# Modulation chunks of the first and last attention layer in halves of 256 columns, one a step

## The chip, the cores and the metric

The kernel runs on one core of a Trainium2 chip. The metric is the device time of one execution in microseconds (us), as the median of several. Five engines work side by side, each through its own list of instructions: PE multiplies matrices, ACT (ScalarE) applies functions and copies, DVE (VectorE) and POOL (GpSimd) do elementwise work, SP (SyncE) issues the transfers (DMAs). They wait for each other only by semaphores. PE's results land in banks of PSUM, everything else lives in SBUF.

## The reference

Four layers over 512 latent and 256 context tokens of width 1024 (batch 1). Layer 0 and layer 3 are of the first kind (multi-head latent attention), layer 1 is a banded window attention (called layer B below), layer 2 a long convolution (layer C). Each layer is modulated by the condition:

```python
for layer in range(DEPTH):
    mx = cond_x @ w_mod[layer] + b_mod[layer]          # cond = silu(c), 1024 -> 3072
    mc = cond_c @ w_mod[layer] + b_mod[layer]
    shift_x, scale_x, gate_x = jnp.split(mx[:, None, :], 3, axis=-1)
    shift_c, scale_c, gate_c = jnp.split(mc, 3, axis=-1)
    hx = rmsnorm(x, g_pre[layer]) * (1.0 + scale_x) + shift_x
    hc = rmsnorm(ctx, g_pre[layer]) * (1.0 + scale_c) + shift_c
    yx, yc = mixer(hx, hc, ...)
    x = x + gate_x * rmsnorm(yx, g_post[layer])
    if with_ctx_out:                                   # not in the last layer
        ctx = ctx + gate_c * rmsnorm(yc, g_post[layer])
```

The mixer of the first kind begins with one projection `h @ w_in`, cut into four: `cq` (512 columns), `ckv` (256), `kr` (64) and a gate (1024). `cq` and `ckv` are normalized (rmsnorm) and multiplied further; the gate goes through SiLU.

## The kernel before

**Modulation.** `w_mod` of a layer is cut into chunks of 512 columns, c = 0 to 5, and each chunk into four blocks of 128x4x256 words, 512 KB each. A chunk is a unit of work: `mod_ab_unit` for scale and shift of the next layer (c = 0 to 3), `mod_g_unit` for the gate of this one (two of them). `mod_chunk` takes the four blocks one after another, does four matmuls for each (each reads 128x256 and writes 32 rows; in the trace a block is x8, a whole unit x32, at L442), all into one bank of PSUM. Then ACT copies the 512 columns out (L455 for scale and shift, L480 for the gate), and for scale and shift PE transposes the copy in four pieces (L459). The units wait in a list, `fillers`, and code of the layers calls `fill()` to put one in: its matmuls need no result of the layer, only their blocks.

**Staging.** Blocks come by two streams, `W` (weights of the layers) and `M` (modulation). `take` gives a block to its reader, and `pump` issues the DMAs of blocks ahead of their readers (L211, on SP's queue), as far as a slot of 1024 words is free in the arena `arena_f` and no more than `cap_d` blocks are staged. A block's slot is free again when its last matmul has read it. A block that isn't staged when its reader is written down is loaded then, into whatever is free. Weights are split into a high and a low part after landing (L230 on ACT, L233 on DVE or POOL), modulation blocks aren't. The low slots of the arena also hold the buffers of the layer (`og`, in layer B the probability buffers `prob` and `sums`), so where a layer's buffers are laid depends on which slots are taken at that moment.

**Layer of the first kind** (`layer_A`). A first loop runs over the six key tiles of 128 tokens: 24 matmuls of 320 columns (L577 to L579) into a bank, then `normed` for 256 of them. `normed` squares and sums on ACT (L715), takes the root and reciprocal in two POOL steps (L358, L359), scales on DVE (L718), transposes on PE (L721) and splits the result. The 64 columns of `kr` are rotated, copied (L757) and transposed (L761). A second loop runs over six cq tiles (four in layer 3): 24 matmuls of 512 columns, then `normed` for 512. A third runs over eight gate blocks, 24 matmuls (L588) for each of the two spans of tokens. Layer 0 has six units to place (four of layer 1's scale and shift, two of its own gate), layer 3 two. `UKS`, `UQ` and `UC` tell from which key tile, cq tile and gate one unit is placed before each step: layer 0 places its six at key tiles 3, 4, 5 and cq tiles 0, 1, 2, layer 3 its two at key tiles 4 and 5. From there on `cap_d` and `look_d` of `M` are 2.

**Order.** The instructions are written in the order of the loops; a scheduler, working from the written order and what each instruction depends on, then sets the order on each engine. What PE meets behind a tile, and so what covers the chain of `normed`, comes out of it. `self.a()` gives the next of a ring of four PSUM banks (pa), `wide` alternates two larger ones (pb).

Of the kernel before, what the change touches and what calls it, by code (L numbers as in the profile page):

```python
# [15 lines left out]
AF = mybir.ActivationFunctionType  # L16
# [4 lines left out]
D = 1024  # L21
# [7 lines left out]
AH = 2  # L29
SU = 2  # L30
WX = {25: (3, 2), 27: (3, 2), 29: (3, 3)}
UKS = (3, 4)
UQ = 0
UC = 0
MC = 2
CH = ((0, 384),)
LS = 2
WD = 3
# [97 lines left out]
class Ring:  # L136
# [6 lines left out]
    def next(self):  # L143
        self.i += 1
        return self.blocks[self.i % len(self.blocks)]
# [125 lines left out]
class Kern:  # L271
# [138 lines left out]
    def want_mod(self, unit):  # L410
        kind, L, c = unit
        w = self.io["w_mod"][L].rearrange("(k p) n -> p k n", p=P)
        if kind == "g":
            c += 4
        for kb in range(4):
            n0, k0 = 512 * c + 256 * (kb // 2), 4 * (kb % 2)
            self.M.want(("mod", L, c, kb), w[:, k0:k0 + 4, n0:n0 + 256], split=False)
# [27 lines left out]
            if kb < 3:  # L445
                yield

    def mod_ab_unit(self, L, c, bank=None):

        nc = self.nc  # L450
        bank = bank or self.a
        ps = bank()
        yield from self.mod_chunk(L, c, ps)
        m = self.fs(512)
        nc.scalar.activation(m.ap, ps, AF.Copy)  # L455
        yield
        ps = bank()
        for b in range(4):
            nc.tensor.transpose(ps[:, P * b:P * b + P], m.ap[:, P * b:P * b + P], self.ident)  # L459
        m.free()  # L460
        part, k0 = c // 2, 4 * (c % 2)
        r = self.col(8).rearrange("p (b s) -> p b s", b=4)
        nc.vector.tensor_reduce(r, ps.rearrange("p (b j s) -> p b s j", b=4, j=4)[:, :, 0:2, :], axis=AX.X, op=ALU.add)
        bm = self.bmod[:, L, 4 * c:4 * c + 4, None].to_broadcast([P, 4, 2])
        if part == 0:
            nc.vector.tensor_tensor(self.ab[:, L, 1, k0:k0 + 4], r, bm, op=ALU.add)
        else:
            nc.vector.scalar_tensor_tensor(r, r, 1.0, bm, op0=ALU.add, op1=ALU.add)
            nc.vector.tensor_tensor(self.ab[:, L, 0, k0:k0 + 4], r, self.gpre[:, L, k0:k0 + 4, None].to_broadcast([P, 4, 2]),
                                    op=ALU.mult)  # L470

    def mod_g_unit(self, L, c, bank=None):

        nc, io = self.nc, self.io
        ps = (bank or self.a)()
        yield from self.mod_chunk(L, 4 + c, ps)
        if c == 0:
            self.mg[L] = self.fs(D)
        m = self.mg[L].ap[:, 512 * c:512 * c + 512]
        nc.scalar.activation(m, ps, AF.Copy)  # L480
        nc.sync.dma_start(out=m[2:3, :], in_=io["b_mod"][L:L + 1, 2048 + 512 * c:2560 + 512 * c])
        yield

# [12 lines left out]
        m.free()  # L496
        return g

    def unit(self, bank=None):
        kind, L, c = self.fillers.pop(0)  # L500
        return (self.mod_ab_unit if kind == "ab" else self.mod_g_unit)(L, c, bank)

    def fill(self, n=1):
        for _ in range(n):
# [197 lines left out]
    def layer_A(self, L, j, h, ctx_out, last):  # L702
        nc, R, F = self.nc, self.R, self.F
# [8 lines left out]
        def normed(ps, n, dst, t):  # L712

            ssq = self.col()
            nc.scalar.activation(self.trash[:, 0:n], ps, AF.Square, accum_out=ssq)  # L715
            self.rstd(ssq, n)
            cn = self.fs(n)
            nc.vector.tensor_scalar(cn.ap, ps, ssq, None, op0=ALU.mult)  # L718
            pt = self.a()
            for k in range(n // P):  # L720
                nc.tensor.transpose(pt[:, P * k:P * k + P], cn.ap[:, P * k:P * k + P], self.ident)  # L721
            cn.free()
            self.split_ps(dst[:, 0, :, P * t:P * t + P], dst[:, 1, :, P * t:P * t + P],
                          pt[:, 0:n].rearrange("p (k n) -> p k n", n=P))

        UK = UKS[0 if ctx_out else 1]
        units = sum(f[:2] in (("ab", L + 1), ("g", L)) for f in self.fillers)

        wide = Banks(self.halves())
        ckv = self.rl(2 * 2 * T)  # L730
# [6 lines left out]
        self.W.pump(4, 3)  # L737
        wk = lambda k: (ws[k // 2][1][0][:, k % 2], ws[k // 2][1][1][:, k % 2])
        for t in order:
            if t == UK:  # L740
                self.M.cap_d = self.M.look_d = MC
            if units and t >= UK:
                self.fill()
                units -= 1
            ps = wide.next()
            self.mm_tok(ps[:, 0:320], h, t, wk, 320)
            normed(ps[:, 0:256], 256, ckvv, t)
            ks = small.next()
            kv4 = ks.v(2, 2, 64)
            if t < 4:  # L750
                kf = self.ropes.next()
                self.rope_ps(kf.v(1, 64), ps[:, 256:320].rearrange("p (a b) -> p a b", a=1), t, 1)
                src = kf.ap[:, 0:64]
            else:
                kf = None
                src = ps[:, 256:320]
            nc.scalar.activation(kv4[:, 0], src[:, None, :].to_broadcast([P, 2, 64]), AF.Copy)  # L757
            nc.vector.tensor_tensor(kv4[:, 1], src[:, None, :].to_broadcast([P, 2, 64]), kv4[:, 0].bitcast(F32), op=ALU.subtract)
            pt = self.a()
            for i in range(2):  # L760
                nc.tensor.transpose(pt[:, P * i:P * i + P], ks.ap[:, P * i:P * i + P].bitcast(F32), self.ident)  # L761
            nc.vector.tensor_copy(krv[:, :, P * t:P * t + P], pt[:, 0:256].rearrange("p (a b) -> p a b", a=2))
# [4 lines left out]
        cqv = cq.v(2, 4, TQ)  # L767
        ws = [self.W.take(("cq", k)) for k in range(0, KD, 2)]
        for t in (order if ctx_out else qt):
            if units and t >= UQ:  # L770
                self.fill()
                units -= 1
            ps = wide.next()
            self.mm_tok(ps, h, t, wk, 512)
            normed(ps, 512, cqv, t)
# [2 lines left out]

        spans = [(0, NX), (NX, NC)] if ctx_out else [(0, NX)]
        for c in range(8):  # L780
            if units and c >= UC:
                self.fill()
                units -= 1
            blk, (wh, wl) = self.W.take(("gate", c))
            outs = [self.a()[:, 0:n] for _, n in spans]
            self.mm_ch(outs, lambda part, k, i: self.h_at(h, part, k, *spans[i]), lambda k: (wh[:, k], wl[:, k]))
            blk.free()
            for (t0, n), o in zip(spans, outs):
                self.gate2(ogv[:, c, t0:t0 + n], o)
        for b in h:  # L790
            b.free()
        self.lo_pool = True
        self.M.cap_d = self.M.look_d = 1

# [152 lines left out]
        units = [(hd, t) for hd in range(8) for t in qt]  # L947
# [891 lines left out]
```

## Time and profile before

| | |
|---|---|
| median of 3 runs | 1951.43 us (1951.01 to 1953.01) |
| the profiled execution | 1952.31 us, span 1950.4 |
| mean granted clock of PE | 0.984 |
| busy: PE, DVE, ACT, POOL | 1818.6, 1169.7, 814.3, 519.7 us |
| waits of PE for modulation blocks in arena_f | 21.6 us in the whole span |
| layer 0's projections | 148 to 312 us |
| layer B's attention | 700 to 985 us |
| layer 3's projections | 1590 to 1715 us |

How to read the rows: a timeline row gives start, duration, engine, line, operation, tiles, shape and count of instructions in a run, and in brackets how long the engine stood idle before it and for what. A row of the waits gives the sum, how often, and the longest. A row of windows gives the window, its length, busy time and (count) of PE, of PE's weight loads, of DVE, ACT and POOL, then the granted clock of PE, the busy share of the DMA engines and GB/s. A row of groups gives the count, busy time and mean duration in ns, then the idle time of the engine before it and what ended it. Rows of SP give when a DMA was issued, and L211 is where both streams issue theirs.

### The profile page before, as it was taken

What the parts mean: (1) busy time and instruction counts of PE and PEld (TensorE: products, weight loads), DVE (VectorE), ACT (ScalarE), POOL (GpSimd) and SP (SyncE); (2) the same over time, 40 slices, a digit from 0 to 9 for tenths busy, and PEclk for the clock granted to TensorE, in tenths of its full rate; (3) what the DMA queues carried; (4) which work ended last, traced back from release to release, by engine and by line L of the source; (5) the groups of instructions that cost most, each with busy time, mean ns of one, the idle gap of its engine ahead of it and who ended that gap; (6) DMA issues with size and microseconds to landing.
All of it is one profiled execution on the core that took longest, in us unless ns stands there. A gap on an engine that the chain in (4) does not pass through costs nothing. (4 is left out here: it accounts for less than half of the span.)

```text
span 1950.4 us, 30304 instructions
## 1 busy us (share of the span) xinstructions
PE 1818.6 (93%) x11628; PEld 1576.9 (81%) x11628; DVE 1169.7 (60%) x2365; ACT 814.3 (42%) x1688; POOL 519.7 (27%) x523
## 2 busy tenths in 40 slices
PE   5879799999999899999989999999989899999998
PEld 3657588999988888888868789999988677889986
DVE  6694134777755277777665456655566553477663
ACT  3473132555544255665654522222222352354451
POOL 5561000000213321222231444444434221000120
PEclk9899999999999999999999999999999899999999
DMA  7867431010133122222363622222222334310121
GB/s 219 261 172 230 150 80 30 23 33 34 55 108 109 55 65 67 77 77 66 107 207 108 200 81 77 76 76 71 72 64 71 107 127 140 97 33 23 44 66 65
DMA packets 186356, 186.31 MB, mean 96 GB/s; under 512 B 16600, under 2 KB 164952, under 8 KB 186212
## 3 DMA queue, kind: packets, MB, share of 16 engines
q1 hardware_dynamic: 186212, 184.39, 30.6%
q8 instruction: 91, 1.49, 0.3%
q14 instruction: 53, 0.43, 0.1%
HBM read 160.24 MB, written 24.12 MB: 95 GB/s over the span
## 5 line engine op out<-in xcount | busy, mean ns | idle before, releaser
L588 PE MATMUL pb<-arena_r 128*128 128x512 f32 (+1 forms) x1488 | 280.9, 342 | 1.9 <-DVE arena_f L567 1.0
L341 ACT ACTIVATE arena_r<-pa 128x384 fp32r<-128x384 f32 (+2 forms) x382 | 175.5, 479 | 206.1 <-PE pa L909 67.9
L588 PEld LDWEIGHTS pb<-arena_r 128*128 128x128 f32 x1488 | 230.1, 190 | 32.9 <-ACT arena_r L1462 1.5
L342 DVE TENSOR_TENSOR arena_r<-pa,arena_r 128x384 fp32r<-128x384 f32 (+2 forms) x382 | 199.5, 536 | 81.7 <-ACT arena_r L341 79.8
L588 PE MATMUL pa<-arena_r,swing_R 128*128 128x512 f32 (+1 forms) x816 | 165.9, 355 | 0.6 <-DVE arena_r L342 0.4
L588 PEld LDWEIGHTS pa<-arena_r,swing_R 128*128 128x128 f32 x816 | 132.2, 188 | 21.8 <-DVE arena_r L342 0.6
L884 PE MATMUL pb<-arena_r 128*128 128x384 f32 (+1 forms) x720 | 141.5, 337 | 3.0 <-ACT arena_r L341 1.8
L606 PE MATMUL pb<-arena_r 128*128 128x512 f32 x552 | 133.7, 394 | 1.6 <-ACT arena_r L230 1.3
L233 POOL TENSOR_TENSOR swing_R<-arena_f,swing_R 128x1024 fp32r<-128x1024 f32 (+1 forms) x33 | 76.2, 2313 | 192.0 <-ACT swing_R L230 142.5
L884 PEld LDWEIGHTS pb<-arena_r 128*128 128x128 f32 x720 | 119.1, 188 | 5.1 <-ACT arena_r L341 2.5
L606 PEld LDWEIGHTS pb<-arena_r 128*128 128x128 f32 x552 | 102.5, 188 | 25.1 <-ACT arena_r L230 1.8
L679 POOL TENSOR_TENSOR arena_f<-arena_f 128x128 f32<-128x128 f32 (+1 forms) x44 | 20.9, 475 | 362.8 <-DVE small L892 178.6
L233 POOL TENSOR_TENSOR arena_r<-swing_F,arena_r 128x1024 fp32r<-128x1024 f32 x36 | 88.0, 2448 | 88.7 <-ACT arena_r L230 83.5
L358 POOL TENSOR_SCALAR small<-small 128x1 f32<-128x1 f32 x68 | 17.8, 261 | 348.0 <-ACT trash L564 139.5
L923 PE MATMUL pa<-arena_r 128*128 128x256 f32 x624 | 91.5, 286 | 2.1 <-DVE arena_r L342 2.1
L923 PEld LDWEIGHTS pa<-arena_r 128*128 128x128 f32 x624 | 81.9, 189 | 4.8 <-ACT arena_r L341 2.5
L1079 PE MATMUL pa<-swing_R,arena_r 128*128 128x256 f32 x576 | 80.3, 289 | 5.0 <-DVE arena_f L348 3.8
L230 ACT ACTIVATE arena_r<-swing_F 128x1024 fp32r<-128x1024 f32 x39 | 41.4, 1063 | 103.9 <-PE pb L588 63.3
L888 DVE TENSOR_REDUCE small<-pb 128x1 f32<-128x768 f32 (+1 forms) x80 | 67.5, 845 | 21.6 <-PE pb L884 20.7
L891 ACT ACTIVATE arena_f<-pb,small 128x768 f32<-128x768 f32 (+1 forms) x80 | 65.2, 817 | 33.1 <-DVE small L889 26.7
L1079 PEld LDWEIGHTS pa<-swing_R,arena_r 128*128 128x128 f32 x576 | 72.9, 192 | 7.3 <-DVE arena_f L348 5.2
L442 PE MATMUL pa<-arena_f,cst 128*32 128x256 f32 x744 | 56.7, 405 | 21.7 <-DMA arena_f<-in_w_mod_dram 21.6
(268 smaller groups left out, 4210.0 us busy)
## 6 DMA issues: line engine op xcount, KB each, us to landing
arena_f<-in_w_mod_dram SPq DMA_DIRECT2D x93, 512.0 KB, 4.7
swing_F<-in_c_w_in_dram SPq DMA_DIRECT2D x31, 512.0 KB, 5.0
kd<-arena_f SPq DMA_DIRECT2D x48, 256.0 KB, 3.5
arena_f<-in_a_w_in_dram SPq DMA_DIRECT2D x24, 512.0 KB, 3.7
arena_f<-kd SPq DMA_DIRECT2D x16, 768.0 KB, 5.2
arena_f<-in_b_w_in_dram SPq DMA_DIRECT2D x20, 512.0 KB, 3.7
x<-arena_f SPq DMA_DIRECT2D x18, 512.0 KB, 4.2
arena_f<-in_a_w_out_dram SPq DMA_DIRECT2D x16, 512.0 KB
```

The source lines that it names most:

```text
L230: nc.scalar.activation(hi, view, AF.Copy)
L233: eng.tensor_tensor(lo, view, hi.bitcast(F32), op=ALU.subtract)
L341: self.nc.scalar.activation(hi, src, AF.Copy)
L342: self.nc.vector.tensor_tensor(lo, src, hi.bitcast(F32), op=ALU.subtract)
L442: nc.tensor.matmul(ps[32 * j:32 * j + 32, n0:n0 + 256], self.cst[:, 4 * kh + j, :], w[:, j, :], start=(kh == 0), stop=(kh == 1), skip_grou ...
L588: nc.tensor.matmul(out, l, rhs(part, k, i), start=(k == 0 and q == 0), stop=(k == kt - 1 and q == 2))
L606: nc.tensor.matmul(ys[:, 512 * hf:512 * hf + 512], ov[:, a, k - ks.start], wt[:, 0, 512 * hf:512 * hf + 512], start=(k == 0 and q == 0), s ...
L884: nc.tensor.matmul(S[:, 512 * b:512 * b + w], l, r[:, k0 + w * b:k0 + w * b + w], start=(q == 0), stop=(q == 4))
L888: nc.vector.tensor_reduce(mx, Sv, axis=AX.XY, op=ALU.max)
L891: nc.scalar.activation(pr.v(nb, w), Sv, AF.Exp, bias=mx, scale=sc, accum_out=sm)
L923: nc.tensor.matmul(o[:, 0:256], vv[:, a_, kt % 3, P * hh:P * hh + P], ptv[i // nh][:, b_, i % nh], start=(i == 0 and q == 0), stop=(i == n ...
L1079: nc.tensor.matmul(ps[:, 0:256], self.h_at(h, part, k, P * t, P), w, start=(k == 0 and i == 0), stop=(k == KD - 1 and i == 2))
```

## The change

A new function does one half of a chunk: two blocks, eight matmuls into a bank of its own, then at once a copy of the 256 columns. The two units get a path that uses it. In `layer_A` a generator runs through all units of the layer, half by half, and one step of it is placed before each cq tile and each gate, none before a key tile. A unit of scale and shift has two steps of matmuls, and its transposes belong to the step that follows. Layer 0 so uses cq tiles 0 to 5 and gates 0 to 5, layer 3 its four cq tiles. `cap_d` of `M` becomes 2 at key tile 4, with a call of `pump`, and 1 at gate 4. Elsewhere (layers B and C) units run whole as before.

```diff
+    def mod_half(self, L, c, half, out):
+        nc = self.nc
+        ps = self.a()
+        for kh in range(2):
+            blk, w = self.M.take(("mod", L, c, 2 * half + kh))
+            for j in range(4):
+                nc.tensor.matmul(ps[32 * j:32 * j + 32, 0:256], self.cst[:, 4 * kh + j, :], w[:, j, :], start=(kh == 0), stop=(kh == 1),
+                                 skip_group_check=True)
+            blk.free()
+        nc.scalar.activation(out[:, 256 * half:256 * half + 256], ps[:, 0:256], AF.Copy)
...
+        if halves:                                    # mod_ab_unit
+            m = self.fs(512)
+            for half in range(2):
+                self.mod_half(L, c, half, m.ap)
+                yield
...
-        UK = UKS[0 if ctx_out else 1]
         units = sum(f[:2] in (("ab", L + 1), ("g", L)) for f in self.fillers)
+        def modulate():
+            for _ in range(units):
+                yield from self.unit(halves=True)
+        mods = modulate()
...
         for t in order:
-            if t == UK:
-                self.M.cap_d = self.M.look_d = MC
-            if units and t >= UK:
-                self.fill()
-                units -= 1
+            if t == 4:
+                self.M.cap_d = self.M.look_d = 2
+                self.M.pump()
...
         for t in (order if ctx_out else qt):
-            if units and t >= UQ:
-                self.fill()
-                units -= 1
+            next(mods, None)
...
         for c in range(8):
-            if units and c >= UC:
-                self.fill()
-                units -= 1
+            if c == 4:
+                self.M.cap_d = self.M.look_d = 1
+            next(mods, None)
...
+        for _ in mods:
+            pass
```

Lines shift by it: a half's matmuls are L451 in the new program and its copy L454, the ab transposes L473, the gate copy L503; whole units elsewhere L438; the tiles L600 to L602, `normed` L738, L741 and L744, the gate matmuls L611, the streams' DMAs L207.

How the scheduler's order comes out, at three places. First PE in layer 0 around the end of key tile 3 (pb_69, 320 columns) and the start of cq tile 0 (pb_69, 512 columns), before:

```order
L577 MATMUL pb_69<-arena_r 128x320
L578 MATMUL pb_69<-arena_r 128x320
L579 MATMUL pb_69<-arena_r 128x320
L442 MATMUL pa_66<-arena_f,cst 32x256 x12
L577 MATMUL pb_70<-arena_r 128x320
L578 MATMUL pb_70<-arena_r 128x320
L579 MATMUL pb_70<-arena_r 128x320
L721 MATMUL pa_68<-ident,arena_f 128x128 x2
L577 MATMUL pb_69<-arena_r 128x512
```
and after:
```order
L600 MATMUL pb_69<-arena_r 128x320
L601 MATMUL pb_69<-arena_r 128x320
L602 MATMUL pb_69<-arena_r 128x320
L744 MATMUL pa_66<-ident,arena_f 128x128 x2
L600 MATMUL pb_69<-arena_r 128x512
```
The three blocks' matmuls that stood between the tile and its transposes are gone from there.

Second, in layer 0 behind a cq tile. PE before, with a whole unit (its L459 are the transposes of the unit ahead):

```order
L579 MATMUL pb_70<-swing_R,arena_r 128x512
L459 MATMUL pa_67<-ident,arena_f 128x128 x4
L442 MATMUL pa_66<-arena_f,cst 32x256 x16
L721 MATMUL pa_68<-ident,arena_f 128x128 x4
L577 MATMUL pb_69<-arena_r 128x512
```
and after, behind a cq tile, with the first matmuls of the next (pb_70) drawn in between:
```order
L602 MATMUL pb_69<-swing_R,arena_r 128x512
L473 MATMUL pa_68<-ident,arena_f 128x128 x2
L602 MATMUL pb_70<-swing_R,arena_r 128x512
L600 MATMUL pb_70<-swing_R,arena_r 128x512
L451 MATMUL pa_65<-arena_f,cst 32x256 x4
L601 MATMUL pb_70<-swing_R,arena_r 128x512
L602 MATMUL pb_70<-swing_R,arena_r 128x512
L744 MATMUL pa_67<-ident,arena_f 128x128 x4
```
SP's queue at the same stage, before (`in_a_w_in` of 128x8x128 are the gate weights):
```order
L211 DMA arena_f<-in_w_mod_dram 128x4x256 x3
L211 DMA arena_f<-in_a_w_in_dram 128x2x512
L211 DMA arena_f<-in_w_mod_dram 128x4x256 x10
L211 DMA arena_f<-in_a_w_in_dram 128x8x128 x2
L211 DMA arena_f<-in_w_mod_dram 128x4x256 x2
L211 DMA arena_f<-in_a_w_in_dram 128x8x128 x2
L211 DMA arena_f<-in_w_mod_dram 128x4x256 x7
L481 DMA arena_f<-in_b_mod_dram 1x512
```
and after:
```order
L207 DMA arena_f<-in_w_mod_dram 128x4x256
L207 DMA arena_f<-in_a_w_in_dram 128x2x512
L207 DMA arena_f<-in_w_mod_dram 128x4x256
L207 DMA arena_f<-in_a_w_in_dram 128x8x128 x2
L207 DMA arena_f<-in_w_mod_dram 128x4x256 x3
L207 DMA arena_f<-in_a_w_in_dram 128x8x128
L207 DMA arena_f<-in_w_mod_dram 128x4x256 x10
L207 DMA arena_f<-in_a_w_in_dram 128x8x128
L207 DMA arena_f<-in_w_mod_dram 128x4x256 x4
L207 DMA arena_f<-in_a_w_in_dram 128x8x128 x2
```
A half stands where a unit stood, one block between the tile and its transposes where four were, and the gate weights are spread between the blocks.

Third, in layer B, whose code is the same, one unit between the steps of its attention (L1143 to L1188, in the new program L1170 to L1215). PE before:

```order
L442 MATMUL pa_65<-arena_f,cst 32x256 x12
L1188 MATMUL pa_66<-arena_r 128x256 x2
L1143 MATMUL pb_69<-arena_r 128x256
L1148 LDWEIGHTS identb
L1148 MATMUL pb_69<-maskb,identb 128x128
L1143 MATMUL pb_69<-arena_r 128x256
L1153 MATMUL pb_70<-arena_r 128x256 x2
L1188 MATMUL pa_66<-arena_r 128x256 x2
L1175 MATMUL pa_67<-ident,arena_f 128x128 x2
L1175 MATMUL pa_68<-ident,arena_f 128x128 x2
L1153 MATMUL pb_69<-arena_r 128x256 x2
L442 MATMUL pa_65<-arena_f,cst 32x256 x4
```
and after:
```order
L438 MATMUL pa_65<-arena_f,cst 32x256 x8
L1180 MATMUL pb_70<-arena_r 128x256 x2
L1170 MATMUL pb_69<-arena_r 128x256
L1175 LDWEIGHTS identb
L1175 MATMUL pb_69<-maskb,identb 128x128
L1170 MATMUL pb_69<-arena_r 128x256
L1202 MATMUL pa_68<-ident,arena_f 128x128 x2
L1116 MATMUL pa_66<-ident,arena_r 128x128 x4
L1180 MATMUL pb_69<-arena_r 128x256 x2
L438 MATMUL pa_65<-arena_f,cst 32x256 x4
L1202 MATMUL pa_66<-ident,arena_f 128x128 x2
L438 MATMUL pa_65<-arena_f,cst 32x256 x4
```
Three blocks of a unit stood together and one came later; now two stand together and two come later. The addresses in the two programs say why: before, layer B's blocks take turns in four slots of the arena, after in three, since `prob` and `sums` were laid over one of the four.

More of the change, by code (lines that the diff above doesn't have):

```diff
@@ L31 @@
 WX = {25: (3, 2), 27: (3, 2), 29: (3, 3)}
[L32 to L35, printed above, removed]
 CH = ((0, 384),)
@@ L446, in mod_chunk, with mod_ab_unit @@
                 yield
-    def mod_ab_unit(self, L, c, bank=None):
+    def mod_half(self, L, c, half, out):
[8 more added lines that the diff above has]
+        nc.scalar.activation(out[:, 256 * half:256 * half + 256], ps[:, 0:256], AF.Copy)
+    def mod_ab_unit(self, L, c, bank=None, halves=False):
         nc = self.nc
         bank = bank or self.a
[L452 to L456, printed above, removed]
+        if halves:
[3 more added lines that the diff above has]
+                yield
+        else:
+            ps = bank()
+            yield from self.mod_chunk(L, c, ps)
+            m = self.fs(512)
+            nc.scalar.activation(m.ap, ps, AF.Copy)
+            yield
         ps = bank()
@@ L470, in mod_ab_unit, with mod_g_unit @@
                                     op=ALU.mult)
-    def mod_g_unit(self, L, c, bank=None):
+    def mod_g_unit(self, L, c, bank=None, halves=False):
         nc, io = self.nc, self.io
[L475 to L480, printed above, removed]
+        if halves:
+            if c == 0:
+                self.mg[L] = self.fs(D)
+            m = self.mg[L].ap[:, 512 * c:512 * c + 512]
+            for half in range(2):
+                self.mod_half(L, 4 + c, half, m)
+                if half == 0:
+                    yield
+        else:
+            ps = (bank or self.a)()
+            yield from self.mod_chunk(L, 4 + c, ps)
+            if c == 0:
+                self.mg[L] = self.fs(D)
+            m = self.mg[L].ap[:, 512 * c:512 * c + 512]
+            nc.scalar.activation(m, ps, AF.Copy)
         nc.sync.dma_start(out=m[2:3, :], in_=io["b_mod"][L:L + 1, 2048 + 512 * c:2560 + 512 * c])
@@ L497, in gates_out, with unit @@
         return g
-    def unit(self, bank=None):
+    def unit(self, bank=None, halves=False):
         kind, L, c = self.fillers.pop(0)
-        return (self.mod_ab_unit if kind == "ab" else self.mod_g_unit)(L, c, bank)
+        return (self.mod_ab_unit if kind == "ab" else self.mod_g_unit)(L, c, bank, halves)
     def fill(self, n=1):
```

## Prediction

> **What bounds the kernel now.** I read the busy shares first, then the waits of PE in the stretches that the change touches, then the timeline around the longest, then SP's timeline to see why it was long.
>
> ```profile
> PE 1818.6 (93%) x11628; PEld 1576.9 (81%) x11628; DVE 1169.7 (60%) x2365; ACT 814.3 (42%) x1688; POOL 519.7 (27%) x523
> ```
> ```profile
> PE pa L442 <- DMA arena_f<-in_w_mod_dram: 9.4, 3, 8.0
> ```
> ```profile
> 199.86 0.66 PE L459 MATMUL pa<-ident,arena_f 128*128 128x128 f32 x4 [1.10 <-ACT arena_f L455]
> 208.48 3.22 PE L442 MATMUL pa<-arena_f,cst 128*32 128x256 f32 x32 [7.96 <-DMA arena_f<-in_w_mod_dram]
> ...
> 220.89 1.07 PE L442 MATMUL pa<-arena_f,cst 128*32 128x256 f32 x16 [1.09 <-DMA arena_f<-in_w_mod_dram]
> 222.28 0.66 PE L721 MATMUL pa<-ident,arena_f 128*128 128x128 f32 x4 [0.31 <-DVE arena_f L718]
> ...
> 230.72 0.66 PE L721 MATMUL pa<-ident,arena_f 128*128 128x128 f32 x4 [0.47 <-DVE arena_f L718]
> ```
> ```profile
> 198.72 2.26 SPq L211 DMA_DIRECT2D arena_f<-in_a_w_in_dram  x2
> 201.06 21.44 SPq L211 DMA_DIRECT2D arena_f<-in_w_mod_dram  x7
> ```
> ```profile
> 208.00:212.00 4.00, 3.52 (x35) 1.73 (x36) 0.75 (x1) 0.18 (x1) 0.00 (x0) 0.61 0.00 0
> ```
> ```profile
> 1619.65 1.93 PE L442 MATMUL pa<-arena_f,cst 128*32 128x256 f32 x32
> ...
> 1621.52 0.44 PE L721 MATMUL pa<-ident,arena_f 128*128 128x128 f32 x2
> ```
>
> PE is the bound, so only time in which PE stands still, or runs slow, can be won. The waits of layer 0's projections (148 to 262 us) hold 9.4 us for modulation blocks, 8.0 of them at one place. SP's rows say why: the block for that place is issued at 201.06, once the transposes of 199.86 have freed a slot of the arena and two gate weights have gone ahead of it; its reader is the next instruction of PE. The matmuls behind the stall run in 3.22 us, the same 32 elsewhere (1619.65) in 1.93: 1.3 us more, at a granted clock of 0.61. (The Trainium skill, "TensorE: Matmul & The Clock Gate", Part 1, says that about 3.4 us without work put the clock to half until about as long a busy stretch has passed; that would be some 1.7 us lost instead of the measured 1.3, an estimate from the page, and the row decides.)
>
> **Part 1: layer 0, what goes.** The whole units leave key tiles 3 to 5 and cq tiles 0 to 2. With them go the two waits for blocks and the short one, 9.4 together; the wait of L459 for its copy (1.10), since the ab transposes now come a step behind the copy; the two waits of L721 (0.31 and 0.47); and the slow clock (1.3). Sum 12.6 us. All blocks but one now have 6 to 10 us of matmuls between the release of their slot and their reader; the stalled one had none.
>
> **Part 2: layer 0, what comes.** A unit of 32 matmuls behind a tile was also cover: behind it the normalization of that tile (ACT, POOL, DVE) was done before PE reached its transposes. Now tiles stand bare, or with a half behind them:
>
> ```profile
> 163.39 0.44 PE L721 MATMUL pa<-ident,arena_f 128*128 128x128 f32 x2 [1.59 <-DVE arena_f L718]
> ```
> ```profile
> 175.60 0.50 PE L577 MATMUL pb<-arena_r 128*128 128x512 f32 x1
> ...
> 179.87 0.40 PE L577 MATMUL pb<-swing_R,arena_r 128*128 128x512 f32 x1
> ```
> ```profile
> L715 ACT ACTIVATE trash<-pb 128x512 bf16<-128x512 f32 x6 | 3.6, 595 | 7.3 <-PE pb L579 7.2
> ...
> L715 ACT ACTIVATION_READ_ACCUMULATOR trash<-pb 128x1 f32 x12 | 2.3, 194 | 0.0
> L715 ACT ACTIVATE trash<-pb 128x256 bf16<-128x256 f32 x6 | 2.3, 384 | 7.4 <-issue 5.1 <-PE pb L579 2.2
> ```
> ```profile
> L718 DVE TENSOR_SCALAR arena_f<-pb,small 128x512 f32<-128x512 f32 x6 | 4.5, 750 | 26.1 <-PE pa L442 15.0 <-POOL small L359 10.4 <-ACT arena_f L347 0.7
> ...
> L718 DVE TENSOR_SCALAR arena_f<-pb,small 128x256 f32<-128x256 f32 x6 | 2.9, 482 | 5.1 <-POOL small L359 4.7 <-PE pa L442 0.3
> ```
> ```profile
> L359 POOL TENSOR_TENSOR small<-small,mhalf 128x1 f32<-128x1 f32 x13 | 7.1, 548 | 1.1
> L358 POOL TENSOR_SCALAR small<-small 128x1 f32<-128x1 f32 x13 | 3.5, 270 | 90.9 <-ACT trash L715 86.5 <-ACT trash L534 3.9
> ```
>
> The chain is square, sum, two POOL steps and scale: 595 + 194 + 270 + 548 + 750 = 2.36 us for a cq tile, 384 + 194 + 270 + 548 + 482 = 1.88 us for a key tile. A matmul of 512 columns takes 0.24 us of PE (the 19th starts 4.27 us after the first), a half of 16 matmuls 1.07 (the row at 220.89), one block half of that.
> - Key tile 3's transposes now follow it at once; the nearest row is 163.39, the same place without a unit: 1.6 us.
> - Key tile 5 has four tile matmuls and a half behind it, 4 x 0.24 + 1.07 = 2.0 against 1.88, with a gate-weight split on ACT that may come first: 0 to 1.5, I take 1.0.
> - Two cq tiles have about 1.7 and 1.5 us behind them against 2.36: 0.7 and 0.9, and what ACT has in hand adds 0.2 each: 0.9 and 1.1. A third lacks 0.75.
> - One block is read some 1.2 us of matmuls after its slot was freed. A transfer takes about 3.7 us from release to use (worked out below), less the 0.75 just before: 1.4 to 1.8, I take 1.4.
> - The eight more copies (16 of 256 columns for 8 of 512) are ACT's, which is busy 42%: no cost but where a square queues behind one, counted above. A half takes a bank of four for itself; up to 0.6 us once, I take 0.3.
>
> Sum 7.1, so layer 0 gains 5.5 us; bounds 9 (the covers suffice, only key tile 3 and the late block remain) and 2 (each chain waits whole). In the gate stage PE was full, so halves there have nothing to fill and nothing to uncover:
>
> ```profile
> 231.00:262.00 31.00, 31.00 (x166) 25.65 (x165) 10.12 (x13) 9.38 (x17) 2.68 (x6) 1.00 0.43 112
> ```
>
> **Part 3: layer B, which the diff does not name.** Its code is the same, but its staging is not. When its probability buffers are allocated, a staged block now sits in a slot that was free before, the buffers go elsewhere, and three slots of 1024 words are left for modulation blocks in place of four. Before, the first three blocks of a unit are staged and the fourth is late; now two are late.
>
> ```profile
> PE pa L442 <- DMA arena_f<-in_w_mod_dram: 4.5, 6, 1.5
> ```
> ```profile
> 722.61 1.50 PE L442 MATMUL pa<-arena_f,cst 128*32 128x256 f32 x24
> ...
> 727.13 0.64 PE L442 MATMUL pa<-arena_f,cst 128*32 128x256 f32 x8 [0.77 <-DMA arena_f<-in_w_mod_dram]
> ```
> ```profile
> 723.31 0.92 SPq L211 DMA_DIRECT2D arena_f<-in_w_mod_dram  x2
> ```
>
> From issue at 723.31 to use at 727.13 are 3.8 us. Counting the instructions of PE between release and use by such rows gives 2.8, 2.6, 3.4, 2.7, 3.4 and 2.8 us for the six late blocks of before, mean 2.95; with the mean wait, 4.5 / 6 = 0.75, a transfer needs 3.7. In the changed program the third blocks have 2.2, 2.0, 3.3, 2.0, 3.2 and 2.0 us, so they wait 1.5, 1.7, 0.4, 1.7, 0.5 and 1.7: 7.5 together. Three of the fourth blocks have 4 us and more and come in time; three have 2.2, and between nothing (the third block's wait ran for them too) and 1.5 each I take the middle, 0.7: 2.1. Less the 4.5 that go, +5.1. While PE stands here, ACT and DVE run on, and some waits for them get shorter; I take back 1.0: **+4**. Bounds 0 (blocks land as fast as their slack) and +9 (the three wait whole). (The Trainium skill, "DMA: Bandwidth & Descriptors", section on the anatomy of one DMA, has a fit of 2.0 us and 436 GB/s: 3.2 us for 512 KB, an estimate. By it layer B would lose only about 1.6. The row at 727.13 says 3.8.) At the end of layer B blocks now come a little earlier:
>
> ```profile
> PE pa L442 <- DMA arena_f<-in_w_mod_dram: 1.4, 3, 0.7
> ```
> Of these 1.4 us (985 to 1110) I count 0.9 as won, between 0 and 1.4.
>
> **Part 4: layer 3.** At 1619.65 a unit covers key tile 4; bare, its transposes wait as at 1609.94, whose tile has no unit behind it:
>
> ```profile
> 1609.94 0.44 PE L721 MATMUL pa<-ident,arena_f 128*128 128x128 f32 x2 [1.78 <-DVE arena_f L718]
> ```
> ```profile
> 1634.49 0.44 PE L721 MATMUL pa<-ident,arena_f 128*128 128x128 f32 x2 [0.77 <-DVE arena_f L718]
> ...
> 1636.87 0.33 PE L761 MATMUL pa<-ident,arena_r 128*128 128x128 f32 x1 [1.94 <-ACT arena_r L757]
> ```
> That is +1.8. The halves among the cq tiles then fill part of the 0.77 and 1.94 behind the last key tile: between 0 and 2.7, I take 1.1. Net +0.7. Layer C reads other slots in the same pattern: no term, 1 us of scatter.
>
> **Sum.** -5.5 + 4.0 - 0.9 + 0.7 = -1.7 us. The profiled execution took 1952.31 (span 1950.4 and 1.9 around it), so 1950.6; the median of the runs shown is 0.9 lower: 1949.7, rounded to **1950**.
>
> **Rivals.** *Faster:* the new waits in layer 0 are not there, and the late blocks of layer B land in their slack. For it: the longest of the six late waits in B was 1.5 us (the row of 4.5), so PE is never far from the landing, and ACT and POOL are free for a chain most of the time (42% and 27% busy). Against it: 163.39 shows what a bare tile costs. Layer 0 -9, B +1, the end of B -0.9, layer 3 0: -9, so 1942.5.
> *Slower, through the queue in layer B:* SP issues in order, and behind the first late block stand weights of layer B. If a block needs 4.7 us from release, the median landing of the page,
>
> ```profile
> arena_f<-in_w_mod_dram SPq DMA_DIRECT2D x93, 512.0 KB, 4.7
> ```
> the third blocks wait 13.5 and three fourth blocks up to 2.5 each, 7.5: 21 less 4.5 is +16.5, in sum about +11, so 1962. It decides from about 4.3 us on: 0.6 more on nine late blocks is 5.4, which brings -1.7 to +3.7, and 0.2%, about what a measurement of this kernel can tell from no change, is 3.9 us. Against it: the 3.8 at 723.31.
> *Nothing won in layer 0:* the stall only moves, because each step now hangs on its own chain: all bare tiles wait the full 1.6 to 2.4 and the late block 3.7, which eats the 12.6. Then +4 from B stands alone: 1955.
>
> **How the numbers follow.** The forecast, a change within 0.2%, has 0.44; faster 0.32; the queue in layer B 0.14; nothing won in layer 0 0.10, most of it slower by over 0.2%. That gives faster 0.32, same 0.46, slower 0.22. The range must leave out no more than 2 in 10: down to 1943, nearly all of the faster case, and up to 1958, the third rival whole and half of the second.
>
> **What would show it.** The waits of PE between 148 and 262 us should have no block over 2 us and no slice of the clock near 0.6 there; new waits for L741 (the scale) at the first two kinds of tiles above; in layer B twelve late blocks with some 9 us of waits in place of six with 4.5. Wrong I am if layer B's waits for blocks stay at 4.5 (then about 1945), or if a late block waits over 2.5 us each time (then over 1955).

## The result, and the profile after

The changed kernel takes 1965.9 us (median of 5, 1960.08 to 1970.22), the kernel before 1951.01 us beside it (median of 5, 1946.31 to 1953.01). The ratio is 1.0084, 95% interval 1.0068 to 1.0101: slower by some 16 us, and outside the predicted range (1943 to 1958). The profiled execution is the one of 1965.9 us.

To see where the 13.6 us between the two profiled executions (1952.31 and 1965.9) went, I cut both traces at the same matmuls, matched by line and number. The rows below are the windows of before and of after: layer 0's projections, from there to the start of layer B's attention, seven of the eight parts of the attention (called the attention below), and its last part with the output projection (called the end). Columns: window, length, busy time (and count) of PE, of its weight loads, of DVE, ACT and POOL, granted clock of PE, busy share of the DMA engines, GB/s.

```profile
148.00:312.00 164.00, 151.16 (x947) 121.48 (x947) 50.79 (x99) 45.01 (x93) 12.46 (x34) 0.97 0.46 136
312.00:700.00 388.00, 373.55 (x2517) 345.13 (x2516) 249.45 (x546) 177.44 (x386) 69.38 (x85) 1.00 0.17 55
700.00:962.00 262.00, 248.81 (x1942) 220.49 (x1941) 187.14 (x489) 153.14 (x403) 61.71 (x75) 0.99 0.26 79
962.00:1105.00 143.00, 135.00 (x808) 103.28 (x807) 81.34 (x154) 74.37 (x154) 43.22 (x48) 0.98 0.55 180
```
```profile
145.60:308.10 162.50, 151.13 (x948) 121.55 (x947) 51.51 (x101) 46.07 (x99) 12.85 (x34) 0.99 0.47 140
308.10:692.30 384.20, 371.73 (x2516) 343.47 (x2515) 250.15 (x546) 177.36 (x386) 69.92 (x85) 1.00 0.17 54
692.30:963.90 271.60, 252.79 (x1942) 219.59 (x1941) 189.07 (x489) 152.40 (x403) 61.56 (x75) 0.99 0.25 77
963.90:1117.80 153.90, 138.94 (x808) 106.78 (x807) 83.82 (x154) 74.36 (x153) 44.33 (x48) 0.94 0.52 170
```

The counts of PE agree to one, so each pair of windows holds the same work. Layer 0's projections, where the change was made, take 162.5 us in place of 164.0 in these two executions. The stretch behind them is 3.8 us shorter. Then layer B's attention is 9.6 us longer (271.6 against 262.0) and its end 10.9 us longer (153.9 against 143.0), 20.5 together, in code that the change does not touch. The start up to 148 us is 2.4 us shorter with the same program. Behind layer B, the last part of layer C (1425 to 1590 us) is 3.1 us longer, and layer 3's projections (1590 to 1700) are 1.8 us shorter.

For layer 0 one execution of each says little. From the first matmul of its projections to the same mark, the four profiled executions with the modulation of before (before and, from the experiments below, b_noslot, b_pad_att and b_pad_end) take 162.6, 166.6, 163.5 and 166.6 us. The five with the halves of the change (after, a_slots, a_l0_s, a_quarter, a_slots_quarter) take 161.1, 163.3, 162.6, 159.8 and 158.7 us: 3.7 less on average. PE's idle time in it is steadier: 12.5 to 14.1 us in the four, 10.4 to 11.4 in the five, 2.4 less on average. The granted clock is 0.95 to 0.98 in the four and 0.97 to 1.00 in the five.

In layer 0 the wait of PE for `normed`'s chain before (148 to 312 us), the waits after (147 to 308 us) and, from the timeline of after, two of the largest:

```profile
PE pa L721 <- DVE arena_f L718: 2.4, 3, 1.6
```
```profile
PE pa L744 <- DVE arena_f L741: 8.3, 8, 2.7
PE pa L451 <- DMA arena_f<-in_w_mod_dram: 1.6, 1, 1.6
```
```profile
172.41 0.44 PE L744 MATMUL pa<-ident,arena_f 128*128 128x128 f32 x2 [2.04 <-DVE arena_f L741]
...
188.19 0.44 PE L744 MATMUL pa<-ident,arena_f 128*128 128x128 f32 x2 [2.75 <-DVE arena_f L741]
```

The stall of 8 us is gone; one block waits 1.6. In its place stand eight waits of transposes for `normed`'s chain, 8.3 us where three took 2.4. The two rows are key tile 3 and key tile 5, the first bare, the second with four matmuls and a half behind it. ACT's timeline tells why the second is so long:

```profile
184.61 1.06 ACT L226 ACTIVATE swing_R<-arena_f 128x1024 fp32r<-128x1024 f32 x1 [4.84 <-DMA arena_f<-in_a_w_in_dram]
185.58 0.37 ACT L738 ACTIVATE trash<-pb 128x256 bf16<-128x256 f32 x1
```

The split of a gate weight stands ahead of the square in ACT's queue and had waited 4.84 us for its transfer; the tile's last matmul was issued at 183.00, its square begins at 185.58.

Slow matmuls are there after the change too. Behind the wait at 172.41 the granted clock is 0.50 for 3.4 us:

```profile
173.20:176.60 3.40, 3.40 (x9) 2.67 (x8) 0.88 (x4) 0.54 (x3) 0.00 (x0) 0.50 0.59 154
```

In layer B's attention the longest waits but those for blocks (4.5 us, shown in Part 3) are, before (700 to 962):

```profile
PE pa L1079 <- DVE arena_f L348: 2.0, 3, 0.7
PE pa L1175 <- ACT arena_r L1090: 1.5, 1, 1.5
```

and after (692.3 to 963.9), longest groups first:

```profile
PE pa L438 <- DMA arena_f<-in_w_mod_dram: 6.9, 7, 1.8
PE pa L1215 <- DVE arena_f L1221: 2.2, 6, 0.7
PE pa L1202 <- DVE arena_f L1188: 1.9, 3, 1.0
PE pb L1170 <- ACT arena_f L1186: 1.7, 3, 0.9
```

Blocks account for 6.9 us where they had 4.5. But PE's idle time in the window grows by 5.6 (271.6 - 252.79 = 18.8 against 262.0 - 248.81 = 13.2), and its busy time by 4.0 for as many matmuls, a sum over runs of matmuls in which short gaps are counted as busy. So the stage loses far more than the 2.4 us by which the wait named after the blocks grew. The other waits, nearly all of the attention's own steps (L1215, L1202 and L1170 are among them), sum to 11.6 us where they had 8.5. These rows do not tell how much of that comes of the late blocks and how much of PE's order, which is another here too.

At the end of layer B the first rows are the longest waits of PE before (962 to 1105; those for blocks are 1.4 and 1.0) and after (964 to 1118), then SP before and after, then DVE before and after, and three rows of PE after:

```profile
PE pa L1175 <- DVE arena_f L1194: 1.4, 2, 0.9
PE pb L588 <- DVE arena_f L567: 1.0, 1, 1.0
```
```profile
PE pb L629 <- DVE arena_f L590: 4.0, 1, 4.0
PE pa L1215 <- ACT arena_r L337: 3.3, 3, 2.1
PE pa L1202 <- DVE arena_f L1188: 3.1, 2, 2.0
PE pb L611 <- DVE arena_f L590: 1.9, 1, 1.9
```
```profile
984.93 16.53 SPq L211 DMA_DIRECT2D arena_f<-in_w_mod_dram  x9
...
1009.75 0.24 SPq L481 DMA_DIRECT2D arena_f<-in_b_mod_dram  x1
```
```profile
1022.28 0.38 SPq L207 DMA_DIRECT2D arena_f<-in_w_mod_dram  x1
...
1031.36 0.25 SPq L504 DMA_DIRECT2D arena_f<-in_b_mod_dram  x1
```
```profile
1024.43 0.69 DVE L495 TENSOR_TENSOR arena_f<-pa,arena_f 128x512 f32<-128x512 f32 x1 [1.99 <-PE pa L494]
```
```profile
1039.58 1.28 DVE L518 TENSOR_TENSOR arena_f<-pa,arena_f 128x512 f32<-128x512 f32 x2
1040.78 1.28 DVE L589 SCALAR_TENSOR_TENSOR pb<-pb,small,arena_f 128x1024 f32<-128x1024 f32 x1
1042.09 1.22 DVE L590 TENSOR_TENSOR arena_f<-arena_f,pb 128x1024 f32<-128x1024 f32 x1
```
```profile
1030.60 7.10 PE L629 MATMUL pb<-arena_r 128*128 128x512 f32 x30
1037.54 1.88 PE L517 MATMUL pa<-arena_f,sel 128*128 128x512 f32 x4
1043.37 1.90 PE L629 MATMUL pb<-swing_R,arena_r 128*128 128x512 f32 x4 [3.95 <-DVE arena_f L590]
```

Read upward from the last row: PE wants to write an output tile, but both large PSUM banks hold tiles that wait for `post` (L589, L590). `post` normalizes a tile, multiplies it by the gate of layer 1 and adds it to x, and the last steps of that gate (L518) start only at 1039.58; before, the last one (L495) at 1024.43. Its bias is issued at 1031.36 (before 1009.75), once the matmuls of the last blocks are done, and those blocks come in ones and twos with other transfers between them, the last at 1022.28, where before nine of them went out in one run from 984.93 to 1001.46. Then PE has a run of 30 output matmuls ahead of L517, the four matmuls that spread the gate over the rows, so these start at 1037.54. In this window idle time grows from 8.0 to 15.0 us. By the waits, output tiles (L629 and L611, before L588) have 6.2 us of it where they had 1.0, the last steps of the attention 8.4 where they had 4.3, blocks 0.3 where they had 2.4. The granted clock falls from 0.98 to 0.94, and the same 808 matmuls take 138.9 us in place of 135.0.

### The profile page after: what moved, and what is told of

It is laid out like the page before. It is cut to its first block, busy times and chain, and to the rows that moved or that the text cites. A ratio compares the mean times of both kernels' runs of the same rounds, so it can differ in the third digit from the quotient of the medians.

```text
span 1964.1 us, 30326 instructions
## 1 busy us (share of the span) xinstructions
PE 1825.0 (93%) x11628; PEld 1576.7 (80%) x11628; DVE 1175.0 (60%) x2365; ACT 814.9 (41%) x1696; POOL 519.4 (26%) x523
## 5 line engine op out<-in xcount | busy, mean ns | idle before, releaser
L611 PE MATMUL pb<-arena_r 128*128 128x512 f32 (+1 forms) x1488 | 280.6, 342 | 3.1 <-DVE arena_f L590 1.9
L611 PEld LDWEIGHTS pb<-arena_r 128*128 128x128 f32 x1488 | 229.2, 189 | 35.0 <-DVE arena_f L590 2.4
L611 PE MATMUL pa<-arena_r,swing_R 128*128 128x512 f32 (+1 forms) x816 | 166.8, 355 | 1.2 <-ACT arena_f L454 0.6
L611 PEld LDWEIGHTS pa<-arena_r,swing_R 128*128 128x128 f32 x816 | 131.9, 188 | 25.4 <-issue 1.6
L629 PE MATMUL pb<-arena_r 128*128 128x512 f32 x552 | 134.0, 394 | 1.9 <-ACT arena_r L226 1.7
L629 PEld LDWEIGHTS pb<-arena_r 128*128 128x128 f32 x552 | 102.2, 188 | 25.4 <-issue 2.0
L629 PE MATMUL pb<-swing_R,arena_r 128*128 128x512 f32 x288 | 75.1, 409 | 4.0 <-DVE arena_f L590 4.0
```

What stands on the lines that cost most here:

```text
L611: nc.tensor.matmul(out, l, rhs(part, k, i), start=(k == 0 and q == 0), stop=(k == kt - 1 and q == 2))
L629: nc.tensor.matmul(ys[:, 512 * hf:512 * hf + 512], ov[:, a, k - ks.start], wt[:, 0, 512 * hf:512 * hf + 512], start=(k == 0 and q == 0), s ...
```

## The experiments

The theory (S): layer B lost one slot of its staging arena, by the accident of which slot a staged weight of its own held when the probability buffers were laid out; the late blocks in its attention and the late gate at its end both come from that. The rival (H): the halves' order as such does it. Each run is timed in five rounds beside the kernel before on the same chip. Layer B has four slots for blocks in its attention (three after the change) and one more in its last part, once the buffer of its rotations is given back; with that one the expectations speak of five.

**The slot given back.** `v, 0` is the third staged weight of layer B; placed in slot 476 it leaves the next one a slot that does not collide.

```diff
-    def slot(self, words, size, turns):
+    def slot(self, words, size, turns, at=None):
+        if at is not None and (self.segs[0][1][at:at + n] < self.BUSY).all():
+            return self._grab(0, at, n, words)
...
-        st = k.fs(words) if must else k.F.slot(words, 1024, k.turns_f)
+        st = k.fs(words) if must else k.F.slot(words, 1024, k.turns_f, 476 if key == ('v', 0) else None)
```

> The changed kernel, with one staged weight of layer B put into the arena slot in which it does not push the probability buffers aside, so that layer B has as many free slots as before the change. Theory S (the loss is the lost slot of layer B, which makes blocks late through its attention and the gate of layer 1 late at its end): the 20 us that layer B and its output projection lost go, about 1946 us (1943 to 1950). Theory H (the loss comes from the halves' order as such, layer B's slots matter little): stays at 1962 to 1968. Between, if only the attention's 9 us hang on the slot and the 11 us at the end have another cause: about 1957.

Measured: 1941.2 us, ratio to before 0.9956 (0.9938 to 0.9973). Theory S, 1.8 us below its range, and more than back to the time of before.

```profile
694.60:954.10 259.50, 247.18 (x1941) 219.18 (x1940) 187.24 (x489) 153.02 (x403) 61.49 (x75) 1.00 0.26 80
954.10:1096.00 141.90, 134.84 (x808) 103.55 (x807) 80.94 (x154) 74.33 (x154) 42.92 (x48) 0.98 0.55 181
```
```profile
976.63 16.48 SPq L209 DMA_DIRECT2D arena_f<-in_w_mod_dram  x9
...
1000.88 0.24 SPq L506 DMA_DIRECT2D arena_f<-in_b_mod_dram  x1
```

The same two windows as above: 259.5 and 141.9 us, no longer than before and 24.1 us less than in the changed kernel, and the nine blocks go out in one run again. In this execution layer 0's projections take 164.7 us, no less than before; of the 11 us between its span (1939.4) and that of before, 4.3 lie between layer 0's projections and layer B's attention, 3.6 in these two windows. Only layer B's part was tested; the rest may hold scatter.

**The slot taken from the kernel before.**

```diff
         prob = Ring(self, "fl", 656, PB)
+        pad = self.fl(384)
         sums = Ring(self, "fl", 256, SU)
...
-        for r in (small, pts, prob, sums):
+        for r in (small, pts, prob, sums, pad):
```

> The kernel before, with 384 unused words laid between layer B's buffers, so that it loses one slot as in the changed kernel; the modulation of layers 0 and 3 is as before. Theory S: about 1971 us (1966 to 1975), with two late blocks a unit. Theory H: 1951, no change. Only the attention hangs on it: about 1960.

Measured: 1976.8 us, ratio 1.0137 (1.0114 to 1.0159), 1.8 us above the range of theory S. It is S from the other side, without a line of the change:

```profile
706.00:975.60 269.60, 251.57 (x1941) 218.86 (x1940) 188.71 (x489) 151.94 (x403) 61.44 (x75) 1.00 0.25 77
975.60:1128.30 152.70, 138.22 (x808) 105.78 (x807) 84.18 (x154) 74.31 (x154) 44.15 (x48) 0.96 0.53 172
```

7.6 and 9.7 us more than before in the two windows. The whole is more than these, 29 us; in this one execution 6 us lie ahead of layer B, in stretches whose program is that of before, so scatter has a part in it, and 3.7 behind its end.

**The same words for the attention only, or for its end only.**

```diff
# b_pad_att: pad as above, given back when the last of eight parts begins
+                    pad.free()
# b_pad_end: no pad; one slot held from there to the end of the attention
+                    pad = self.F.slot(1024, 1024, 6)
```

> The kernel before with the 384 unused words between layer B's buffers, given back at the start of the last of the eight parts of its attention: the slot is missing for six units of modulation, and there again for the last blocks and the output projection. If the two losses (some 9 us in the attention, some 11 us at its end) are separate: about 1957 us, layer B's attention 9 us longer, its end as before. If the late end follows from the attention (blocks that lag from unit to unit): 1968 to 1976 as in b_noslot.

> The kernel before with one slot of 1024 words held from the start of the last part of layer B's attention until its end: missing only for the last blocks. If the end has a loss of its own (the gate of layer 1 late, so that the output tiles wait for it in PSUM): 1956 to 1968. If the loss at the end follows from the attention: 1948, no change.

Measured: 1962.63 us, ratio 1.0077 (1.0057 to 1.0097), and 1959.0 us, ratio 1.0058 (1.0039 to 1.0076). The windows, first of the run with the pad in the attention, then of the one with the slot held at the end:

```profile
697.10:968.00 270.90, 252.98 (x1940) 219.72 (x1940) 188.61 (x489) 151.92 (x403) 61.33 (x75) 0.99 0.24 77
968.00:1120.30 152.30, 138.21 (x808) 106.76 (x807) 84.31 (x154) 73.31 (x153) 43.06 (x48) 0.94 0.54 174
```
```profile
703.90:965.40 261.50, 247.21 (x1942) 219.18 (x1941) 187.37 (x489) 153.19 (x403) 61.84 (x75) 1.00 0.25 77
965.40:1116.90 151.50, 135.57 (x808) 104.30 (x807) 81.73 (x154) 74.61 (x153) 43.38 (x48) 0.97 0.54 174
```

The first run does not do what its expectation says. `sums` was laid behind the pad and stays there, across a slot, when the pad is given back, and the 384 words that come back are no slot of 1024. So the slot is missing at the end too, as in b_noslot; in the trace its blocks go out in runs of at most three from 975 us on, the last at 1025.22. This run repeats b_noslot in layer B (8.9 and 9.3 us more than before, against 7.6 and 9.7) and says nothing of an end that has its slot back. The second run does its part: with the slot there the attention is as short as before (261.5), and with the slot missing only behind it the end is 8.5 us longer. So the loss at the end needs no attention that lagged; whether a lagging attention alone would delay the end is not tested.

b_pad_att and b_noslot lose the same in layer B and yet differ by 14 us. Between their profiled executions 9 us lie ahead of layer B, and 9.3 in the last part of layer C, which takes 161.9 and 171.2 us (165.0 before, 168.1 after). No run was about that stretch, and what sets its length is open.

**Late blocks, or PE's order?** With a slot less, the order of PE in layer B changes too, not only when blocks land. The first of these runs was meant to keep that order nearly and to make the blocks small.

```diff
+        elif key[0] == "mod" and (key[1], key[2] // 4) in ((2, 0), (3, 0)):
+            k.nc.sync.dma_start(out=view[:, 0:1], in_=src[:, 0:1])
```

> The changed kernel, in which the modulation blocks that layer B takes in its attention (scale and shift of layers 2 and 3) are loaded only to a quarter, 128 KB in place of 512; the rest of each slot keeps what was there, so the modulation of those layers is not computed. Layer B still has one slot less, and PE's order around its units is nearly that of the changed kernel. If the loss in layer B is the lateness of blocks: most of the 9 us in the attention and some of the end go, 1942 to 1950. If it is PE's order with the units in more pieces (less cover between the attention's own steps): 1956 to 1964.

> The same quarter loads with layer B's slots as in a_slots, so the modulation of layers 2 and 3 is not computed here either. It bounds what more slots could still bring: the six late blocks that remain wait some 4.5 us. If a late block costs its wait alone: 1936 to 1938. If it also holds the queue of PE and with it the attention's chains: 1930 to 1935. If nothing is left to win there: 1941.

Measured: 1953.14 us, ratio 1.0023 (1.0007 to 1.0038), and 1953.76 us, ratio 1.0029 (1.0017 to 1.0042).

```profile
689.40:952.30 262.90, 249.47 (x1941) 219.44 (x1940) 188.21 (x489) 151.02 (x402) 62.14 (x75) 1.00 0.13 39
952.30:1101.10 148.80, 138.31 (x808) 106.24 (x807) 81.02 (x155) 75.14 (x154) 43.36 (x48) 0.94 0.50 163
```
```profile
689.30:948.60 259.30, 247.55 (x1934) 218.78 (x1933) 187.34 (x485) 150.84 (x400) 60.92 (x75) 1.00 0.13 39
948.60:1101.40 152.80, 139.97 (x816) 107.18 (x815) 86.50 (x158) 75.09 (x155) 42.92 (x48) 0.96 0.49 158
```

In the first run the attention takes 262.9 us, 8.7 less than in the changed kernel, and of the end's 10.9 us 5.1 go. The total, 1953.1, is 3 us above the range of the first case and below that of the second. But the order is not kept. The first unit of the attention, in the changed kernel and in this run:

```profile
714.94 1.07 PE L438 MATMUL pa<-arena_f,cst 128*32 128x256 f32 x16
719.56 0.64 PE L438 MATMUL pa<-arena_f,cst 128*32 128x256 f32 x8 [0.86 <-DMA arena_f<-in_w_mod_dram]
724.52 0.64 PE L438 MATMUL pa<-arena_f,cst 128*32 128x256 f32 x8 [1.25 <-DMA arena_f<-in_w_mod_dram]
```
```profile
712.02 1.07 PE L440 MATMUL pa<-arena_f,cst 128*32 128x256 f32 x16
715.71 1.07 PE L440 MATMUL pa<-arena_f,cst 128*32 128x256 f32 x16
```

The changed kernel takes two blocks, one and one, this run two and two: only the size of the transfers was changed, and the scheduler made another order of it. So the run shows that the loss hangs on how long a block takes to come. It does not separate PE's waits for late blocks from the order that the scheduler builds around them; that stays open. The second run missed all three expectations: the attention gains 0.2 us only, and the end loses 10.9. One block's matmuls (8 of the 816) moved there, and the units are placed otherwise. With every slot in place its end is about as long as with one missing, so the placement can cost that much too. It does not tell what more slots would bring; that stays open.

**Halves or whole units, and layer 3.**

```diff
# a_whole_s, on top of a_slots
-                yield from self.unit(halves=True)
+                for _ in self.unit():
+                    pass
+                yield
+                yield
# a_l0_s, on top of a_slots: layer 3's two units whole at key tiles 4 and 5
-            for _ in range(units):
+            for _ in range(units if ctx_out else 0):
```

> The changed kernel with layer B's slots as in a_slots, but each unit runs whole at every second step in place of a half at each step. If the halves themselves bring the gain in layer 0 (shorter stretches between tiles, blocks spread): 3 to 6 us slower than a_slots. If the gain comes from placing the work over more steps, whole or not: within 2 us of a_slots.

> The changed kernel with layer B's slots as in a_slots, and layer 3's two units placed whole at key tiles 4 and 5 as before the change: halves in layer 0 alone. If layer 3's part is worth what the two traces show (1.8 us there): 1 to 2 us slower than a_slots. If it is worth nothing: the same within 1 us.

Measured: whole units over the same steps 1946.39 us, ratio 0.9987 (0.9973 to 1.0); halves in layer 0 alone 1942.65 us, ratio 0.996 (0.9944 to 0.9976). The first is 5 us slower than a_slots, as its first case said, but the traces do not put that where the case did. In layer 0's projections the run with whole units takes 161.2 us against 163.3 of a_slots, with 1.4 us more idle time of PE (11.9 against 10.5). Of the 5.0 us between the two profiled executions 3.0 lie in the last part of layer C (167.6 against 164.6) and 1.8 in layer 3 (110.5 against 108.7). So the number came out by luck, and a gain of 5 us from halves in layer 0 is not shown.

The second is 1.5 us slower than a_slots, as its first case said, but within the scatter (0.9956 with layer 3's part). Nor does its trace show the part: its layer 3, with whole units, takes 107.2 us, that of a_slots 108.7.

**Covering the bare key tiles.** The halves begin earlier, at key tile 5, 4 or 3. a_k5 places `v, 0` in slot 412, a_k4 does too, a_k3 needs no such help.

```diff
-            if t == 4:
+            if t == (5 if ctx_out else 4):        # a_k3: 3, a_k4: 4
                 self.M.cap_d = self.M.look_d = 2
                 self.M.pump()
+            if t >= (5 if ctx_out else 4):        # a_k3: 3, a_k4: 4
+                next(mods, None)
```

> The changed kernel with the halves begun at key tile 3 in place of the first cq tile (layer 3: key tile 4), nothing staged ahead from gate 2 until layer 0's attention has its buffers; layer B has its five slots. If bare key tiles cost what a_slots shows (2.04 and 2.67 us in layer 0): 2 to 5 us faster than a_slots, about 1938. If the earlier steps find their blocks late instead (the DMA engines are busy 95% until 167 us): no faster, 1941 to 1947.

> As a_slots, with one step of the halves at key tile 5 (layer 3: from key tile 4) and the rest behind it: five slots in layer B. Covers of bare tiles as above: 1 to 3 us faster than a_slots for layer 0 and layer 3 together. If what is taken from the gates' steps is missed nowhere and nothing is covered: the same as a_slots within 1 us.

> The changed kernel with the halves begun at key tile 4 in both layers, nothing staged ahead from gate 1 until layer 0's attention has its buffers, five slots in layer B. Key tile 3 stays bare (2.04 us in a_slots), key tile 5 is covered: by that about 1936, as a_k5. If each step that moves forward covers more: 1933 or less. If the blocks come late at the earlier steps, as in a_k3: 1938 to 1941.

> a_k5 once more, on one chip with a_k4, to tell whether its lead over a_slots holds: ratio to before 0.992 to 0.996 if so; above 0.996 if it was scatter.

Measured: a_k3 1938.27 us, ratio 0.9946 (0.9929 to 0.9964); a_k5 1935.66, ratio 0.9939 (0.992 to 0.9957); a_k4 1941.35, ratio 0.9964 (0.995 to 0.9978); a_k5 again 1936.18, ratio 0.9943 (0.9923 to 0.9962). The intervals overlap each other and that of a_slots, so the order among the kernels is not settled, though a_k5 came out lowest twice; its repeat lies in the range expected if its lead holds. a_k4 came out 0.4 us above the range of its last case, late blocks. Layer 0's projections in a_k5:

```profile
145.40:304.60 159.20, 151.10 (x948) 121.73 (x947) 51.40 (x101) 45.60 (x99) 12.79 (x34) 0.99 0.49 143
```

Idle time in them is 8.1 us (159.2 - 151.1), against 12.8 before and 11.4 after. a_k5 beats both kernels: 0.6% faster than the one before.

## Why the prediction was wrong

- **What goes in layer 0** (Part 1): right as to the stalls: the long one is gone, and one block waits 1.6 us. The 1.3 us for slow matmuls were not won in this execution: PE is busy 151.1 us in both, since after has its own 3.4 us at a clock of 0.50, behind key tile 3. The sign "no slice of the clock near 0.6 there" did not hold.
- **What comes in layer 0** (Part 2): the mechanism was right, and the sizes too small. Key tile 3 waited 2.04 for the 1.6 of the prediction, key tile 5 2.75 for 1.0 (the gate-weight split that I had let come first did come first, and late, since it waited for its own transfer), the late block 1.6 for 1.4. The stage won 1.5 us in these two executions in place of 5.5; over nine executions 3.7, of which 2.4 are idle time of PE.
- **The attention of layer B** (Part 3): the step that failed is "while PE stands here, ACT and DVE run on, and some waits for them get shorter; I take back 1.0". It had the wrong sign: the other waits grew by 3.1 us, and PE's busy time by 4.0. Blocks cost 2.4 us more (6.9 in seven waits against 4.5 in six, where twelve late blocks were forecast), half of the +5.1 that I had; the stage lost 9.6, above the bound of +9 that had been meant for blocks that wait whole. That all of it comes of the missing slot is shown from both sides, by a_slots and b_noslot. Within it, Part 3 priced the waits for blocks alone and put PE's new order in layer B, which stands in the section on the change, at nothing. A likely road is that behind a matmul that waits for a block stand the transposes and products from which DVE and ACT get their work; how the other 7 us divide between this and the order itself is not shown. (The fit that Part 3 quotes from the Trainium skill, "DMA: Bandwidth & Descriptors", is, by its section's heading, one of transfers issued from GpSimd, while SP issues these; the sum did not use it.)
- **The end of layer B**: the second step that failed, and the larger one. I looked at the waits for blocks there, counted 0.9 us of them as won (they fell by 2.1), and did not ask who waits for what the blocks compute. The gate of layer 1 is needed by the first output tile, and with two PSUM banks for output tiles PE stands when the gate is late: 5.2 us more there, 4.1 more in the last steps of the attention, 3.9 more busy time, +10.9 in all. b_pad_end shows that the slot missing in this part alone costs 8.5.
- **Between 312 and 700**: 3.8 us were won that I had not foreseen. The kernel with the slot given back has them too (383.7 us there), and b_noslot, with the program of before, has not (389.1). The clock does not explain it: before has a stretch at a lower one in it (0.91 from 660 to 680 us), but a_slots has one too (0.98 from 594.6 to 694.6). The cause is open.
- **Layer 3** (Part 4): +0.7 was forecast. The two executions show 1.8 us less (108.2 against 110.0), but b_noslot and a_l0_s, whose layer 3 is that of before, take 108.4 and 107.2, so the change has no part in it that can be told.
- **Layer C**: "no term, 1 us of scatter". Its last part came out 3.1 us longer, and ranges from 161.9 to 171.2 us over the runs; the cause is open.
- **The rivals**: the slower one had the right place, layer B, and the wrong road. The waits for blocks sum to 6.9 us in the attention, not to the 21 that it had; the rest of the price was in the attention's own steps, PE's busy time and the end.

Summed over the two windows, layer B has +20.5 where the prediction had +3.1: 17.4 us, more than the miss of 16. Layer 0's shortfall of 4 in these executions is met by the 3.8 won behind it, and the 2.4 at the start make up the rest.

## What to carry to other kernels

When buffers and staging slots share one arena, a change in one layer can take a slot from another: compare the layout of every later stage before its cost is called nothing, and pin it if the time hangs on it. Price a late operand not by its own wait alone: look at what stands behind the waiting instruction in its queue, at what other order the scheduler makes, and at who waits for what is computed from it. When an experiment is to take a buffer away and give it back, check in the layout that what comes back is usable. An interleaved unit of work is also cover for the chain in front of it: before it is moved, list what it covered.

## What the runs showed of the hardware

A late stretch is paid twice. At the end of layer B idle time rose by 7.0 us, and the same 808 matmuls took 3.9 us more at a granted clock of 0.94 in place of 0.98; in the run with the pad in the attention too, the clock there was 0.94 and PE's busy time 138.2 us. At the ends of before and a_slots the clock is 0.98 and the busy time 135.0 and 134.8. After the change the clock there is at 0.50 or 0.51 in four stretches (989.0 to 995.8, 1002.6 to 1006.0, 1043.6 to 1047.0 and 1105.0 to 1108.4 us); before, at 0.50 from 986.0 to 992.8. The third lies around the longest wait, 3.95 us up to 1043.37. Around the first two no wait is over 2.2 us, but in the 3.4 us ahead of the first PE is busy for 1.7.

(The Trainium skill, "TensorE: Matmul & The Clock Gate", Part 1, has the clock at half after at least one idle window of about 3.4 us. The stretch at 1043.6 agrees; those at 989.0 and 1002.6 came with shorter waits, so here the measurement decides.)

The same program does not take the same time in every execution, and PE's idle time is the steadier measure of a stage: in layer 0's projections, five executions of the same code differ by 4.6 us in length and by 1.0 in idle time.
